# Expert weights in loads of 1 MB with 8 KB rows, expert 1's gather ahead of expert 0's first product, and the turned inner activations copied ahead of the evacuated rows

## The chip, the core and the metric

The kernel runs on one core of a Trainium2 chip. The core has five engines, each with its own queue of instructions: TensorE (PE) for matrix products and transposes, VectorE (DVE), ScalarE (ACT), GpSimd (POOL) and SyncE (SP), which here only issues transfers. Sixteen DMA engines move data between memory and the on-chip buffers. The metric is the time of one execution in microseconds. Before the change it is 886.41 us, the median of three runs (886.3 to 887.85).

## The reference

One layer of a decoder: 512 tokens of width 1024, fp32.

```python
h = layer_norm(x)
proj = h @ w_in                       # nine parts
y_a = hgrn2_branch(...) @ w_branch_a; y_b = stick_breaking_branch(...) @ w_branch_b
h = layer_norm(alpha*h + (sigmoid(gate_a)*y_a + sigmoid(gate_b)*y_b) @ w_mix_out)
h = layer_norm(alpha*h + memory_cross_attention(h, mem, ...))
h = layer_norm(alpha*h + hierarchical_moe(h, ...))

# hierarchical_moe: top-1 of 4 groups, top-2 of the 4 experts in it
for e in range(16):
    hidden = silu(h @ w1[e]) * (h @ w3[e])       # 1024 -> 512
    y = y + combine[:, e:e+1] * (hidden @ w2[e]) # 512 -> 1024
```

The reference lets every expert see every token with a weight that is zero for most; a kernel may compute the chosen tokens alone. One expert has 6 MB of weights in fp32, all sixteen 96 MB.

## The kernel before

The layer runs stage after stage: entry norm and projections, the two branches, their mixing, the cross attention, the experts, the last norm. The change touches the experts, from some 584 us on, and the buffers that weights are loaded into.

**Weights.** The class `Weights` holds a list of loads in the order of their use (`add`) and a list of free buffers (`raw_free`). Whenever a buffer comes free (`buffers`, `done`), `load` issues the next load on SP's queue (L54). A load is 512 KB, 4 KB on each of 128 partitions: for `w1` and `w3` two rows of 2 KB that lie side by side in memory (for expert 0 apart), for `w2` one row of 4 KB. Twelve loads make one expert. The buffers are slots of earlier stages (`raws`, `ring`, `ringout`, `xres`, `sbk`, `wx`, `s`), each given to the list when its stage has done with it. Eight loads can be under way; each further issue waits for the landing of the eighth before it.

**Routing.** For each tile of 128 tokens the router's scores are made (`route_*`), the chosen experts and the places of the tokens in the experts' lists. The tokens of expert 0 are turned by one-hot products (`gather0`, L1129) and copied to `xgT` (L1260). For the others, `count_tokens` (L1272) and `sums` (L1135) make lists of token numbers on PE from one-hot matrices that DVE writes (`one_hots`, L1117); `gather(e)` (L1187) then fetches the rows of expert e's tokens from `x2d` in memory with an indirect DMA of POOL's queue. The rows of the last tile are stored to `x2d` on ACT's queue (L1250), and POOL's queue stores scaled rows to `yd` (`route_base`, L1058), to which the experts' outputs are later added.

**Side work.** `tell()` is a generator of small steps; `begin` puts it beside the products and `tick()` lets it go on after a part of a product. So counting, sums and `gather(1)` stand in the middle of expert 0's first product.

**The loop over experts.** Round e has, in the code's order: `up(e)` (L1451; beyond 64 tokens also L1462), `turn_in(e+1)` (PE L1424, copies L1425 on ACT and DVE), `gather(e+2)`, `down(e-1)` (L1492; beyond 64 tokens L1500), `to_rows(e-1)` and its scatter, and `turn_hidden(e)`: four transposes on PE (L1479) and a copy on DVE (L1481) into the tile that `down(e)` of the next round reads. `to_rows` scales the output out of the product's banks into rows: ACT L1515 twice and L1521 four times, DVE L1523 four times. The rows lie in one buffer (`y_out`), which the scatter (L1301, an indirect DMA with addition, on POOL's queue) reads; the next expert's `to_rows` has to wait until that scatter has landed. Each engine takes its instructions in this order, so what stands behind a waiting instruction waits too.

**The tail.** After expert 15's first product, `yd` is read back (L1559) and added up with the outputs of experts 14 and 15, which are not scattered (L1591, L1624), and the last norm ends the kernel.

Of the kernel before, what the change touches and what calls it, by code (L numbers as in the profile page):

```python
# [24 lines left out]
class Weights:  # L25


    def __init__(self, nc, ahead):
        self.nc, self.ahead = nc, ahead
        self.other = ()  # L30
        self.src, self.raw_free, self.raw, self.parts = [], [], {}, {}
        self.out_free, self.own = [], {}
        self.kept = None
        self.plain = set()
        self.loaded = self.split = 0
        self.limit = 1 << 30
# [8 lines left out]

    def buffers(self, raw=(), out=()):
        self.raw_free += raw
        self.out_free += out
        self.load()

    def load(self):
        while self.raw_free and self.loaded < len(self.src):
            ap, buf = self.src[self.loaded], self.raw_free.pop(0)
            self.nc.sync.dma_start(buf.rearrange("p (k n) -> p k n", n=ap.shape[-1]), ap)  # L54
            self.raw[self.loaded] = buf
            self.loaded += 1

    def prepare(self, upto):
        while self.split <= min(upto, self.limit, len(self.src) - 1):
            j = self.split  # L60
            if not self.out_free:
                return
            hi, lo = self.own[j] = self.out_free.pop(0)
            raw = self.raw.pop(j)
            self.nc.scalar.copy(hi, raw)  # L65
            eng = self.nc.gpsimd if j in self.other else self.nc.vector
            eng.tensor_tensor(lo, raw, hi.bitcast(F32), op=ALU.subtract)  # L67
            n = self.src[j].shape[-1]
            self.parts[j] = tuple(a.rearrange("p (k n) -> p k n", n=n) for a in (hi, lo))
            self.split += 1  # L70
            self.raw_free.append(raw)
            self.load()

    def get(self, j):
        if j in self.plain:
            return self.raw[j]
        self.prepare(j + self.ahead)
        return self.parts[j]

    def done(self, j):  # L80
        if j in self.plain:
            self.raw_free.append(self.raw.pop(j))
# [14 lines left out]
def tile_kernel(ctx, tc, x, mem, ln_in_g, ln_in_b, w_in, hg_lb_logits, hg_norm_g, w_branch_a, w_branch_b,  # L97
# [75 lines left out]
    W.buffers([raws[:, i] for i in range(2)], outs)  # L173
    nc.sync.dma_start(xres[:, 1], x[P:2 * P])
    W.buffers([raws[:, i] for i in (2, 3)])
# [272 lines left out]
    wx = pp.tile([P, 2, T], F32, name="wx")  # L448
    sbk = pp.tile([P, 2, T + 1], F32, name="sbk")
# [263 lines left out]
    W.buffers([sbk.rearrange("p a n -> p (a n)")[:, 0:D]], [out_tile(3)])  # L713
# [176 lines left out]
    def ring(tags):  # L890
        for i in tags:
            r = slot(i, [P, 2, D], name=f"ring{i}")
            rings[i] = [r[:, 0], r[:, 1]]
            W.buffers(rings[i])
# [81 lines left out]
    W.buffers([s8[:, 1], wx.rearrange("p a n -> p (a n)")])  # L976
# [255 lines left out]

    natural_major([q_wo[1]], oc(0), oc(1), ev_wo, before=lambda t: begin(route_first(t), 2))
    for i in range(4):
        r = pp.tile([P, 2, D], F32, tag=f"out{i}", name=f"ringout{i}")
        W.buffers([r[:, 0], r[:, 1]])
# [6 lines left out]
    gather0(0, 0)  # L1243
    gather0(0, 1)
    route_fold(t)
    W.buffers([xres[:, 0]])
# [6 lines left out]
    route_place(slice(t, t + 1))  # L1253
    gather0(3, 0)
    gather0(3, 1)
    s3 = slot(3, [P, 2, D], name="s3")
    W.buffers([s3[:, 1]])
    xgT = s3[:, 0].rearrange("p (k n) -> p k n", n=P)
# [3 lines left out]
    W.buffers([xres[:, 1]])  # L1262
# [123 lines left out]
    route_base(t)  # L1386
    route_told(slice(2, 4))
    one_hots()

    def tell():  # L1390
        count_tokens()
        sums(told[:, 0:NE], [(r, t, k) for r, t in all_rt for k in range(2)])
        nc.vector.tensor_scalar(gidx, told[:, 0:NE], 4096.0, None, op0=ALU.add)
        gather(1)
        yield 1
        W.buffers([xres[:, 2], xres[:, 3]])
        count_blocks()
        nc.vector.tensor_copy(tok, told[:, 0:NE])
        yield 0.5
        yield from route_gates()  # L1400
# [18 lines left out]
    def turn_in(e):  # L1419
        xg = gbr[:, 1].rearrange("t (q p k) -> t q k p", q=4, k=2)  # L1420
        for q in range(2):
            p = msp()
            for i in range(4):
                nc.tensor.transpose(p[:, i * P:(i + 1) * P], xg[:, 2 * q + i // 2, i % 2], ident)  # L1424
# [18 lines left out]
    def up(e):  # L1443
        x, (a, b) = xgT, sums_up
        ws = []
        for q, js in enumerate(q_up[e]):
            ws.append([W.get(j) for j in js])
            for k in range(2):
                c = 2 * q + k
                for i, w in enumerate(reversed(ws[q])):  # L1450
                    nc.tensor.matmul(a[64 * i:64 * i + 64], x[:, c, 0:64], w[:, k * 512:(k + 1) * 512], start=c == 0,  # L1451
                                     stop=c == 7)
            tick()
        if e == 0:
            finish()
        beyond[e] = nc.tensor.value_load(tally[0:1, e:e + 1], min_val=0, max_val=T)

        def part(g):
            for c in range(8):
                for i in range(4):  # L1460
                    o = c % 2 * 512 + i % 2 * 256
                    nc.tensor.matmul(b[32 * i:32 * i + 32, 256 * g:256 * g + 256],  # L1462
                                     x[:, c, 64 + 32 * g:96 + 32 * g], ws[c // 2][i // 2][:, o:o + 256],
                                     start=c == 0, stop=c == 7)
# [11 lines left out]
    def turn_hidden(e, h, p=None):  # L1476
        p = p or msp()
        for i in range(4):
            nc.tensor.transpose(p[:, i * P:(i + 1) * P], h[:, i * P:(i + 1) * P], ident)  # L1479
# [4 lines left out]
    def down(e):  # L1484

        x, (a, b) = hT.pop(e), sums_down
        ws = [W.get(j) for j in q_w2[e]]

        def base():
            for k, w in enumerate(ws):  # L1490
                for n in range(2):
                    nc.tensor.matmul(a[64 * n:64 * n + 64], x[:, k, 0:64], w[:, n * 512:(n + 1) * 512], start=k == 0,  # L1492
                                     stop=k == 3)
                tick()

        def part(g):
            for k, w in enumerate(ws):
                s = slice(64 + 32 * (k // 2), 96 + 32 * (k // 2))
                for i in range(4):
                    nc.tensor.matmul(b[32 * i:32 * i + 32, 256 * g:256 * g + 256], x[:, 2 * g + k % 2, s],  # L1500
                                     w[:, 256 * i:256 * i + 256], start=k == 0, stop=k == 3)
# [24 lines left out]
    for e in range(NE - 1):  # L1526
# [4 lines left out]
        if e == 13:  # L1531
            scratch.extend(W.raw_free.pop() for i in range(4))
            more_blocks()
            W.buffers(scratch)
# [17 lines left out]
    def last_loads():  # L1552

        assert W.loaded == len(W.src)
        whole = [i for i in rings if all(any(b is f for f in W.raw_free) for b in rings[i])][:4]
        free.extend(b for b in W.raw_free if b is not s3[:, 1] and not any(b is h for i in whole for h in rings[i]))
# [50 lines left out]
    yh[NE - 1], yl[NE - 1] = two_parts(3, "yg15")  # L1607
# [3 lines left out]
    p = msp()  # L1611
    for i in range(4):
        nc.tensor.transpose(p[:, i * P:(i + 1) * P], h[:, i * P:(i + 1) * P], ident)
# [7 lines left out]
    ws = [W.get(j) for j in q_w2[NE - 1]]  # L1621
    for n in range(2):
        for k, w in enumerate(ws):
            nc.tensor.matmul(sums_up[n], x[:, k], w[:, halves[n]], start=k == 0, stop=k == 3)  # L1624
# [96 lines left out]
```

## Time and profile before

| | us |
|---|---|
| median of three runs | 886.41 |
| profiled execution | 886.88 |
| its span | 885.1 |
| PE busy | 847.2 (96%) |
| DVE busy | 457.1 (52%) |
| ACT busy | 337.7 (38%) |
| POOL busy | 123.8 (14%) |

The span is what the trace covers; the profiled execution's own time is 1.8 us longer. Mean granted clock of PE: 0.985. Of 177.66 MB moved, 157.31 MB are SP's queue (56144 packets), which is the weights for the most part.

How to read it: a busy engine is not yet the bound, and a wait of an engine that nobody waits for costs nothing. A row of the timeline gives the start and the length of a group of like instructions, and in brackets how long the engine stood idle before it and what ended that. In the rows of stretches, the bracketed counts are instructions, and PEclk is the granted clock as a share of full speed.

### The profile page before, as it was taken

The numbers are of one execution on the slowest core, as the hardware profiler recorded it, in microseconds if no ns is written. First come the engines' busy times: TensorE is split into PE (matmuls) and PEld (weight loads), VectorE is DVE, ScalarE is ACT, GpSimd is POOL, SyncE is SP. The second block draws the span as 40 slices with busy tenths as digits, with TensorE's granted clock in tenths as the row PEclk, the third lists the DMA queues.
The fourth block names the chain that finished last, engine by engine and source line by source line (L and its number), as shares of the span: only waits on it lengthen the run. The fifth ranks groups of instructions, "written<-read, shape, count | busy, mean of one in ns | idle before, by whom it ended". The sixth has DMA issues, their size and how long they took to land. (4 is left out here: it accounts for less than half of the span.)

```text
span 885.1 us, 13705 instructions
## 1 busy us (share of the span) xinstructions
PE 847.2 (96%) x5296; PEld 586.1 (66%) x5296; DVE 457.1 (52%) x806; ACT 337.7 (38%) x640; POOL 123.8 (14%) x212
## 2 busy tenths in 40 slices
PE   6999999999999999999999999997989999999994
PEld 5888777788777777888988888773333343344343
DVE  6632578644558554759744566684242322422336
ACT  2332336543554553422633444222332333323234
POOL 5400000000212220002200000221121111211102
PEclk8999999999999999999999999999999999999998
DMA  8443222222212227332742567599999999999952
GB/s 299 140 135 96 73 93 76 72 72 72 95 48 72 72 78 256 119 118 73 219 167 70 187 220 284 215 351 373 392 378 364 346 350 351 359 360 357 361 172 95
DMA packets 63908, 177.66 MB, mean 201 GB/s; under 512 B 7797, under 2 KB 7829, under 8 KB 63824
## 3 DMA queue, kind: packets, MB, share of 16 engines
q1 hardware_dynamic: 56144, 157.31, 49.6%
q0 software_dynamic: 7536, 18.65, 6.9%
q8 instruction: 60, 0.98, 0.4%
q10 hardware_dynamic: 144, 0.52, 0.1%
q14 instruction: 24, 0.20, 0.1%
HBM read 168.47 MB, written 15.73 MB: 208 GB/s over the span
## 5 line engine op out<-in xcount | busy, mean ns | idle before, releaser
L1523 DVE TENSOR_SCALAR ringgb<-I-5383_acc,wgb 32x256 f32<-32x256 f32 x60 | 29.2, 487 | 118.2 <-ACT ringgb L1521 116.7
L1451 PE MATMUL I-5377_acc<-ring,s 128*64 128x512 f32 x276 | 79.0, 596 | 0.0
L1515 ACT ACTIVATE ringgb<-I-5381_acc,wgb 64x512 f32<-64x512 f32 x30 | 20.5, 684 | 80.8 <-DMA yd<-ringgb,s 64.9
L67 DVE TENSOR_TENSOR I-69_out<-raws,I-69_out 128x1024 fp32r<-128x1024 f32 x24 | 29.4, 1224 | 38.3 <-ACT I-69_out L65 37.9
L1451 PEld LDWEIGHTS I-5377_acc<-ring,s 128*64 128x64 f32 x276 | 23.7, 137 | 34.0 <-issue 31.5
L1301 POOL DMA_INDIRECT yd<-ringgb,s x14 | 22.4, 1600 | 157.1 <-DVE I-8384w2k L1481 16.9
L663 DVE TENSOR_TENSOR_SCAN wx<-sbk 128x128 f32<-128x128 f32 (+3 forms) x32 | 27.1, 847 | 28.7 <-POOL sbk L659 28.7
L65 ACT CAST I-73_out<-raws 128x1024 fp32r<-128x1024 f32 x23 | 24.2, 1050 | 45.5 <-PE I-3558_acc L190 17.1
L67 DVE TENSOR_TENSOR I-71_out<-raws,I-71_out 128x1024 fp32r<-128x1024 f32 x23 | 28.1, 1224 | 24.6 <-ACT I-71_out L65 24.6
L65 ACT CAST I-69_out<-raws 128x1024 fp32r<-128x1024 f32 x25 | 26.3, 1050 | 32.7 <-issue 9.2
L67 DVE TENSOR_TENSOR I-73_out<-raws,I-73_out 128x1024 fp32r<-128x1024 f32 x22 | 26.9, 1223 | 16.1 <-ACT I-73_out L65 15.8
L65 ACT CAST I-71_out<-raws 128x1024 fp32r<-128x1024 f32 x24 | 25.3, 1054 | 24.9 <-PE I-384_acc L189 4.6
L1521 ACT ACTIVATE ringgb<-I-5383_acc,wgb 32x256 f32<-32x256 f32 x60 | 27.9, 464 | 4.3 <-issue 2.2
L1451 PE MATMUL I-5377_acc<-raws,s 128*64 128x512 f32 x60 | 27.8, 601 | 0.0
L659 POOL TENSOR_SCALAR_AFFINE_SELECT sbk<-sbk 128x128 f32<-128x128 f32 x32 | 14.3, 447 | 94.5 <-ACT sbk L654 50.2
L1462 PE MATMUL I-5379_acc<-ring,s 128*32 128x256 f32 x392 | 27.4, 380 | 0.0
L1451 PE MATMUL I-5377_acc<-ringout,s 128*64 128x512 f32 x92 | 25.0, 595 | 0.0
L1187 POOL DMA_INDIRECT ringgb<-x2d,s x15 | 15.7, 1045 | 49.3 <-PE I-5540_ms L1424 8.6
L1462 PEld LDWEIGHTS I-5379_acc<-ring,s 128*32 128x32 f32 x392 | 14.5, 110 | 12.1 <-issue 4.1
L216 POOL TENSOR_TENSOR I-1461hgss<-I-1461hgss,mhalf 128x4 f32<-128x4 f32 x1 | 1.0, 1047 | 136.9 <-DVE I-1461hgss L567 136.9
L966 POOL MEMSET I-4794w2k<- 128x128 f32 x1 | 0.2, 204 | 109.9 <-PE I-4740_ms L190 109.9
L1451 PEld LDWEIGHTS I-5377_acc<-ringout,s 128*64 128x64 f32 x92 | 7.6, 137 | 11.4 <-issue 11.1
(3506 smaller groups left out, 2410.3 us busy)
## 6 DMA issues: line engine op xcount, KB each, us to landing
ring<-in_moe_w_dram SPq DMA_DIRECT2D x107, 512.0 KB, 11.9
raws<-in_w_in_dram SPq DMA_DIRECT2D x44, 512.0 KB, 3.5
ringout<-in_moe_w_dram SPq DMA_DIRECT2D x32, 512.0 KB, 13.2
raws<-in_moe_w_dram SPq DMA_DIRECT2D x20, 512.0 KB, 11.2
xres<-in_moe_w_dram SPq DMA_DIRECT2D x16, 512.0 KB, 13.7
s<-in_moe_w_dram SPq DMA_DIRECT2D x8, 512.0 KB, 13.0
raws<-in_xa_wk_dram SPq DMA_DIRECT2D x7, 512.0 KB, 3.7
raws<-in_xa_wv_dram SPq DMA_DIRECT2D x7, 512.0 KB, 3.7
```

What stands on the lines that cost most here:

```text
L65: self.nc.scalar.copy(hi, raw)
L67: eng.tensor_tensor(lo, raw, hi.bitcast(F32), op=ALU.subtract)
L216: nc.gpsimd.tensor_tensor(o, v, mhalf[:, :v.shape[-1]], op=ALU.pow)
L659: nc.gpsimd.affine_select(kp[:, d], kp[:, d], pattern=[[-1, P]], compare_op=ALU.is_gt, fill=1.0, base=w * (P - 1), channel_multiplier=1 - ...
L663: nc.vector.tensor_tensor_scan(rest[:, :n][:, ::-1], kp[:, n:0:-1], kp[:, n:0:-1], 1.0, ALU.mult, ALU.bypass)
L1187: nc.gpsimd.indirect_dma_start(out=gbr[:, 1], out_offset=None, in_=x2d[:, :], in_offset=bass.IndirectOffsetOnAxis(ap=gidx[:, e:e + 1], axi ...
L1301: nc.gpsimd.indirect_dma_start(out=yd[:, :], out_offset=bass.IndirectOffsetOnAxis(ap=idx, axis=0), in_=y, in_offset=None, bounds_check=T - ...
L1451: nc.tensor.matmul(a[64 * i:64 * i + 64], x[:, c, 0:64], w[:, k * 512:(k + 1) * 512], start=c == 0, stop=c == 7)
L1462: nc.tensor.matmul(b[32 * i:32 * i + 32, 256 * g:256 * g + 256], x[:, c, 64 + 32 * g:96 + 32 * g], ws[c // 2][i // 2][:, o:o + 256], start ...
L1515: nc.scalar.activation(y[0:64, n * 512:(n + 1) * 512], a[s], AF.Copy, scale=gates_at[s, 0, e:e + 1])
L1521: nc.scalar.activation(o, z, AF.Copy, scale=f)
L1523: nc.vector.tensor_scalar(o, z, f, None, op0=ALU.mult)
```

## The change

It has three parts.

**Loads of 1 MB.** The expert weights are loaded in 6 pieces for each expert instead of 12, 8 KB on each partition: for `w1` and `w3` four rows of 2 KB side by side (expert 0's still apart), for `w2` two of 4 KB. 192 loads become 96. Buffers of 2048 columns are given whole, and `halve`, `free` and `room` cut one into two for the loads of other stages that are 4 KB wide, and put two halves together again when both are free. `wx` and `sbk` become one tile. The sum of the buffers stays. The order of rows in a product follows the new layout (`turn_in`, `turned_hidden` take other strides), and `xgT` moves to another slot.

**Expert 1's gather first.** `route_told` and `one_hots` of the last tile come before the copies of `xgT`; `tell()` is driven to its first `yield` before `up(0)`, so that counting, sums and `gather(1)` stand ahead of expert 0's first product, and `route_base` of the last tile, with its two stores to `yd`, comes after the gather.

On POOL, around the last two stores to `yd` of the routing (`yd<-w2k`) and the first gather (`ringgb<-x2d`), the order before is:

```order
L1058 DMA yd<-I-5263w2k 128x512
L1058 DMA yd<-I-5267w2k 128x512
L1265 IOTA wgb 128x48
L1266 IOTA wgb 128x48
L1058 DMA yd<-I-5355w2k 128x512
L1058 DMA yd<-I-5359w2k 128x512
L1187 DMA ringgb<-x2d,s_4897 128x1024
```

and with the change:

```order
L1099 DMA yd<-I-5242w2k 128x512
L1099 DMA yd<-I-5246w2k 128x512
L1308 IOTA wgb 128x48
L1309 IOTA wgb 128x48
L1228 DMA ringgb<-x2d,s_4884 128x1024
L1099 DMA yd<-I-5388w2k 128x512
L1099 DMA yd<-I-5392w2k 128x512
```

The first gather has moved ahead of the last two stores; nothing else on this queue has.

**The copy before the evacuations.** `turn_hidden(e)` stands right behind `down(e-1)`, ahead of `to_rows(e-1)` and the scatter.

On DVE, one round of the loop before; the four `TENSOR_SCALAR` to `ringgb` are the evacuation of `to_rows`, the `COPY` to `w2k` is that of `turn_hidden`, the `COPY` to `s` that of `turn_in`:

```order
L1473 TENSOR_TENSOR I-5896w2k<-I-5896w2k,I-5377_acc 64x512
L1473 TENSOR_TENSOR I-5896w2k<-I-5896w2k,I-5379_acc 64x512
L1425 COPY s_5346<-I-5909_ms 128x512
L1438 UNCONDITIONAL_BRANCH
L1523 TENSOR_SCALAR ringgb<-I-5383_acc,wgb 32x256 x4
L1481 COPY I-5984w2k<-I-5978_ms 128x512
```

and with the change:

```order
L1516 TENSOR_TENSOR I-5859w2k<-I-5859w2k,I-5374_acc 64x512
L1516 TENSOR_TENSOR I-5859w2k<-I-5859w2k,I-5376_acc 64x512
L1466 COPY s_4884<-I-5872_ms 128x512
L1481 UNCONDITIONAL_BRANCH
L1529 COPY I-5932w2k<-I-5926_ms 128x512
L1572 TENSOR_SCALAR ringgb<-I-5380_acc,wgb 32x256 x4
```

The copy of the turned inner activations has passed the evacuation. On PE the four transposes stand behind the down product as before, since the evacuation has nothing on PE.

```diff
 class Weights:
+    def halve(self, wide):
+        if id(wide) not in self.halves_of:
+            a, b = wide[:, 0:1024], wide[:, 1024:2048]
+            self.halves_of[id(wide)] = a, b
+            self.pair[id(a)], self.pair[id(b)] = (wide, b), (wide, a)
+        return self.halves_of[id(wide)]
+    def free(self, buf):
+        wide, other = self.pair.get(id(buf), (None, None))
+        if wide is not None and self.is_free(other):
+            self.raw_free = [b for b in self.raw_free if b is not other] + [wide]
+        else:
+            self.raw_free.append(buf)
+    def room(self, wide):
+        fit = [b for b in self.raw_free if not wide or b.shape[-1] == 2048]
...
+        if wide or fit[0].shape[-1] == 1024:
+            return fit[0]
+        buf, other = self.halve(fit[0])
+        self.raw_free.insert(0, other)
+        return buf
     def load(self):
-        while self.raw_free and self.loaded < len(self.src):
-            ap, buf = self.src[self.loaded], self.raw_free.pop(0)
-            self.nc.sync.dma_start(buf.rearrange("p (k n) -> p k n", n=ap.shape[-1]), ap)
+        while self.loaded < len(self.src):
+            ap = self.src[self.loaded]
+            k, n = ap.shape[1:]
+            buf = self.room(k * n == 2048)
+            if buf is None:
+                return
+            self.nc.sync.dma_start(buf.rearrange("p (k n) -> p k n", n=n), ap)
...
-            q_up[e] = [tuple(W.add(w[0, e, 2 * q * P:(2 * q + 2) * P].rearrange("(k p) n -> p k n", p=P) if e == 0 else
-                                   w[0, e, 2 * q * P:(2 * q + 2) * P].rearrange("(p k) n -> p (k n)", k=2)[:, None], True)
-                             for w in (moe_w1, moe_w3)) for q in range(4)]
+            q_up[e] = [tuple(W.add(w[0, e, 4 * q * P:(4 * q + 4) * P].rearrange("(k p) n -> p k n", p=P) if e == 0 else
+                                   w[0, e, 4 * q * P:(4 * q + 4) * P].rearrange("(p k) n -> p (k n)", k=4)[:, None], True)
+                             for w in (moe_w1, moe_w3)) for q in range(2)]
         if e > 0:
-            q_w2[e - 1] = [W.add(moe_w2[0, e - 1, k * P:(k + 1) * P].rearrange("(k p) n -> p k n", p=P), True)
-                           for k in range(4)]
+            q_w2[e - 1] = [W.add(moe_w2[0, e - 1, 2 * q * P:(2 * q + 2) * P].rearrange("(p k) n -> p (k n)", k=2)[:, None],
+                                 True) for q in range(2)]
...
     route_place(slice(t, t + 1))
+    route_told(slice(2, 4))
+    one_hots()
     gather0(3, 0)
...
-    route_base(t)
-    route_told(slice(2, 4))
-    one_hots()
     def tell():
         count_tokens()
         sums(told[:, 0:NE], [(r, t, k) for r, t in all_rt for k in range(2)])
         nc.vector.tensor_scalar(gidx, told[:, 0:NE], 4096.0, None, op0=ALU.add)
         gather(1)
+        yield 0
+        route_base(t)
+        W.buffers([xrow[1]])
         yield 1
-        W.buffers([xres[:, 2], xres[:, 3]])
         count_blocks()
...
-    begin(tell(), 2)
+    telling = tell()
+    next(telling)
+    begin(telling, 1)
...
     def up(e):
...
+        for c in range(8):
+            for i in range(2):
+                nc.tensor.matmul(a[64 * i:64 * i + 64], x[:, c, 0:64], w(1 - i, c, 0, 512), start=c == 0, stop=c == 7)
+            if c % 2:
+                tick()
...
         if e > 0:
             for step in down(e - 1):
                 step()
+        turn_hidden(e, h)
+        if e > 0:
             finish()
             scatter(to_rows(e - 1), gidx[:, e - 1:e])
-        turn_hidden(e, h)
```

## Rows read from the trace of the kernel before

**Rows 1.** page, part 2: busy tenths in 40 slices of 22.1 us

```profile
PE   6999999999999999999999999997989999999994
...
DMA  8443222222212227332742567599999999999952
```

**Rows 2.** stretches of the expert loop, base products of line 1451 alone

```profile
624.20:666.80 42.60, 21.26 (x96) 6.63 (x96) 0.96 1.01 383
666.80:749.40 82.60, 35.44 (x160) 11.04 (x160) 1.00 0.98 353
749.40:776.20 26.80, 14.18 (x64) 4.42 (x64) 1.00 0.98 358
776.20:835.60 59.40, 21.26 (x96) 6.63 (x96) 1.00 0.99 360
```

**Rows 3.** timeline 589 to 610 us: start, us, engine, line, operation, [idle before <- releaser]

```profile
589.94 0.35 ACTq L1250 DMA_DIRECT2D x2d<-xres  x1
...
595.03 0.69 DVE L1260 COPY s<-I-5280_acc 128x512 f32<-128x512 f32 x1 [2.14 <-PE I-5280_acc L1129]
...
596.04 1.38 DVE L1117 TENSOR_SCALAR I-5366w2k<-s 128x128 bf16<-128x128 bf16 x8
...
599.68 1.11 POOL L1187 DMA_INDIRECT ringgb<-x2d,s  x1 [3.03 <-DVE wgb L1278]
...
607.11 1.13 PE L1424 MATMUL I-5533_ms<-ident,ringgb 128*128 128x128 f32 x4 [4.35 <-DMA ringgb<-x2d,s]
```

**Rows 4.** one stretch, all engines: busy us and count of each, PEclk, DMA, GB/s

```profile
607.00:610.00 3.00, 2.90 (x14) 2.57 (x16) 0.72 (x2) 0.59 (x1) 0.64 (x1) 0.50 1.03 414
```

**Rows 5.** timeline 643 to 667 us, around the down products of experts 2 and 3

```profile
645.44 1.61 POOL L1301 DMA_INDIRECT yd<-ringgb,s  x1 [11.29 <-DVE I-5984w2k L1481]
...
645.65 1.08 PE L1492 MATMUL I-5381_acc<-s,I-5984w2k 128*64 128x512 f32 x4
...
646.55 2.75 PE L1492 MATMUL I-5381_acc<-xres,I-5984w2k 128*64 128x512 f32 x12
...
654.51 1.39 ACT L1515 ACTIVATE ringgb<-I-5381_acc,wgb 64x512 f32<-64x512 f32 x2 [8.43 <-DMA yd<-ringgb,s]
...
655.92 1.93 ACT L1521 ACTIVATE ringgb<-I-5383_acc,wgb 32x256 f32<-32x256 f32 x4
...
657.89 2.04 DVE L1523 TENSOR_SCALAR ringgb<-I-5383_acc,wgb 32x256 f32<-32x256 f32 x4 [10.35 <-ACT ringgb L1521]
...
659.97 0.69 DVE L1481 COPY I-6174w2k<-I-6168_ms 128x512 f32<-128x512 f32 x1
...
660.76 1.36 PE L1492 MATMUL I-5381_acc<-ring,I-6174w2k 128*64 128x512 f32 x4 [2.15 <-issue]
...
663.55 2.56 PE L1492 MATMUL I-5381_acc<-ring,I-6174w2k 128*64 128x512 f32 x8
```

**Rows 6.** timeline 770.5 to 777 us, the down product of expert 10

```profile
771.36 1.22 PE L1492 MATMUL I-5381_acc<-raws,I-7504w2k 128*64 128x512 f32 x3 [0.38 <-ACT s L1425]
...
772.78 2.79 PE L1492 MATMUL I-5381_acc<-ring,I-7504w2k 128*64 128x512 f32 x11
```

**Rows 7.** scatters of line 1301: issue to landing

```profile
DMA to landing us min/median/max: 8.2/9.0/9.9
```

**Rows 8.** DMA from 584 to 842 us: queue, packets, MB, share; then issues

```profile
q1 hardware_dynamic: 22975, 83.67, 84.9%
...
q10 hardware_dynamic: 144, 0.52, 0.5%
...
x2d<-xres ACTq DMA_DIRECT2D x1, 512.0 KB, 7.3
```

**Rows 9.** DMA from 338 to 340.4 us, two queues busy

```profile
q0 software_dynamic: 153, 0.63, 64.0%
q1 hardware_dynamic: 158, 0.32, 37.0%
```

**Rows 10.** DMA issues from 560 to 580 us, KB each, median us to landing

```profile
x2d<-xres POOLq DMA_DIRECT2D x2, 512.0 KB, 3.1
```

More of the change, by code (lines that the diff above doesn't have):

```diff
@@ L172, in tile_kernel @@
     outs = [out_tile(i) for i in range(4)]
-    W.buffers([raws[:, i] for i in range(2)], outs)
+    raw2 = [raws[:, i:i + 2].rearrange("p a n -> p (a n)") for i in (0, 2)]
+    W.buffers([raw2[0]], outs)
     nc.sync.dma_start(xres[:, 1], x[P:2 * P])
-    W.buffers([raws[:, i] for i in (2, 3)])
+    W.buffers([raw2[1]])
     for t in (2, 3):
@@ L447, in tile_kernel @@
     G = slot(10, [P, NT, 512], name="hgG")
-    wx = pp.tile([P, 2, T], F32, name="wx")
-    sbk = pp.tile([P, 2, T + 1], F32, name="sbk")
+    wsb = pp.tile([P, 4 * T + 2], F32, name="wsb")
+    wx = wsb[:, 0:2 * T].rearrange("p (a n) -> p a n", a=2)
+    sbk = wsb[:, 2 * T:4 * T + 2].rearrange("p (a n) -> p a n", a=2)
+    wsb = W.halve(wsb[:, 0:4 * T])
     oTa_h = oTa_l = None
@@ L891, in ring @@
         for i in tags:
-            r = slot(i, [P, 2, D], name=f"ring{i}")
-            rings[i] = [r[:, 0], r[:, 1]]
-            W.buffers(rings[i])
+            rings[i] = slot(i, [P, 2 * D], name=f"ring{i}")
+            W.buffers([rings[i]])
     rings, attended = {}, []
@@ L1231, in tile_kernel @@
     more = take([10], I32, where=1)
+    xrow = [xres[:, t:t + 2].rearrange("p a n -> p (a n)") for t in (0, 2)]
     natural_major([q_wo[1]], oc(0), oc(1), ev_wo, before=lambda t: begin(route_first(t), 2))
     for i in range(4):
-        r = pp.tile([P, 2, D], F32, tag=f"out{i}", name=f"ringout{i}")
-        W.buffers([r[:, 0], r[:, 1]])
+        W.buffers([pp.tile([P, 2 * D], F32, tag=f"out{i}", name=f"ringout{i}")])
     gather0(1, 0)
@@ L1444, in up, with w @@
         x, (a, b) = xgT, sums_up
[L1445 to L1453, printed above, removed]
+        def w(i, c, o, n):
+            return W.cut(q_up[e][c // 4][i], c % 4 * 512 + o, n)
+        for c in range(8):
[3 more added lines that the diff above has]
+                tick()
         if e == 0:
@@ L1486, in down, with w @@
         x, (a, b) = hT.pop(e), sums_down
-        ws = [W.get(j) for j in q_w2[e]]
+        def w(k, o, n):
+            return W.cut(q_w2[e][k // 2], k % 2 * D + o, n)
         def base():
-            for k, w in enumerate(ws):
+            for k in range(4):
                 for n in range(2):
-                    nc.tensor.matmul(a[64 * n:64 * n + 64], x[:, k, 0:64], w[:, n * 512:(n + 1) * 512], start=k == 0,
-                                     stop=k == 3)
+                    nc.tensor.matmul(a[64 * n:64 * n + 64], x[:, k, 0:64], w(k, n * 512, 512), start=k == 0, stop=k == 3)
                 tick()
         def part(g):
-            for k, w in enumerate(ws):
+            for k in range(4):
                 s = slice(64 + 32 * (k // 2), 96 + 32 * (k // 2))
@@ L1531, in tile_kernel @@
         if e == 13:
-            scratch.extend(W.raw_free.pop() for i in range(4))
+            lent = [b for b in W.raw_free if b.shape[-1] == 2048][-2:]
+            W.raw_free = [b for b in W.raw_free if not any(b is i for i in lent)]
+            scratch.extend(h for b in lent for h in W.halve(b))
             more_blocks()
-            W.buffers(scratch)
+            W.buffers(lent)
         if e == 0:
@@ L1554, in last_loads @@
         assert W.loaded == len(W.src)
-        whole = [i for i in rings if all(any(b is f for f in W.raw_free) for b in rings[i])][:4]
-        free.extend(b for b in W.raw_free if b is not s3[:, 1] and not any(b is h for i in whole for h in rings[i]))
+        whole = [i for i in rings if W.is_free(rings[i])][:5]
+        for b in W.raw_free:
+            if not any(b is rings[i] for i in whole):
+                free.extend(W.halve(b) if b.shape[-1] == 2048 else [b])
+        free.append(s8[:, 1])
         for t in (1, 2, 3, 0):
@@ L1606, in tile_kernel @@
     yh[NE - 2], yl[NE - 2] = two_parts(rooms.pop(), "yg14")
-    yh[NE - 1], yl[NE - 1] = two_parts(3, "yg15")
+    yh[NE - 1], yl[NE - 1] = two_parts(rooms.pop(), "yg15")
     base, rest = down(NE - 2)
     base()
-    p = msp()
-    for i in range(4):
-        nc.tensor.transpose(p[:, i * P:(i + 1) * P], h[:, i * P:(i + 1) * P], ident)
+    p = turned_hidden(h)
     x = work("w2k", [P, T], bufs=5).rearrange("p (k n) -> p k n", n=P)
@@ L1620, in tile_kernel @@
     rest()
-    ws = [W.get(j) for j in q_w2[NE - 1]]
     for n in range(2):
-        for k, w in enumerate(ws):
-            nc.tensor.matmul(sums_up[n], x[:, k], w[:, halves[n]], start=k == 0, stop=k == 3)
+        for k in range(4):
+            nc.tensor.matmul(sums_up[n], x[:, k], W.cut(q_w2[NE - 1][k // 2], k % 2 * D + n * T, T), start=k == 0, stop=k == 3)
     for j in q_w2[NE - 1]:
```

52 lines of the change are left out of this document (31 added, 21 removed).

## The prediction

> **What bounds the kernel now.** I read the page's slices first: TensorE (PE) is at nine tenths or more in all slices but four, and from the 27th slice (575 us) to the 38th (841 us) the 16 DMA engines are full too [rows 1]. So two things are nearly bounds in the expert stage, and it is the waits of PE that tell which one ends last. The view by stretches shows how fast PE goes through the experts: 96 base products (32 an expert) in 42.6 us, then 160 in 82.6, 64 in 26.8 and 96 in 59.4 [rows 2]. A round is thus 14.2, 16.5, 13.4 and 19.8 us; the long ones are experts with more than 64 tokens.
>
> PE's own waits are few. Before expert 1 it stands 4.35 us for that expert's gather, issued at 599.68 and landed at about 607.1; in the stretch behind, the granted clock is 0.50, the lower of the two levels (1.2 of 2.4 GHz), until 610 [rows 3, 4]. At 660.76 it has stood 2.15 us ahead of a down product [rows 5]. What ended last there is seen on the other engines: ACT's evacuation waits 8.43 us for the scatter of the expert before, then takes 1.39 + 1.93; DVE's evacuation follows with 2.04, and only then DVE copies the turned inner activations that the down product reads (659.97 + 0.69 = 660.66) [rows 5]. The row names "issue" as the releaser; the copy's end, 0.1 us before the product starts, tells more. A small wait at the same place of the loop, 0.38, stands at 771.36 [rows 6]. These are the waits of the stage that I price.
>
> Behind that lies a loop that PE doesn't see in most rounds: scatter to landing 9.0 (8.2 to 9.9) [rows 7], 1.39 + 1.93 on ACT, 2.04 on DVE, 0.69 for the copy that the scatter also waits for (its releaser is DVE L1481), and some 0.2 of issue: 15.3; from the scatter at 645.44 to the end of the next copy, 660.66, it is 15.2 [rows 5]. In the three rounds up to 666.8 PE without its stalls needs (42.6 - 3.85) / 3 = 12.9 us, so the loop falls behind by 2.4 a round, 7.1 in three, and PE loses 2.15 of it: some 5.0 us of lateness are absorbed. In longer rounds the loop catches up.
>
> **The change, part by part.**
>
> *The copy ahead of the evacuations.* The copy no longer stands behind 2.04 on DVE, and so not behind ACT's 1.39 + 1.93 and the scatter. Both waits of this kind go: 2.15, and 1.70 of clock (the down product behind it takes 663.55 + 2.56 - 660.76 = 5.35 instead of 645.65 to 649.30 = 3.65) [rows 5]; 0.38, and 772.78 + 2.79 - 771.36 - 3.65 = 0.56 [rows 6]. Together **-4.8**. What is late next is the bank of the down product itself: ACT L1515 has to empty it before the next down product writes it. That comes 1.93 + 2.04 + 0.69 = 4.66 earlier than the old condition, so the absorbed lateness rises from 5.0 to about 9.6. The loop loses the copy's 0.69: 14.6 at unchanged landings. If an expert beyond 64 tokens follows, the second bank has to be emptied too, but such rounds are the long ones.
>
> *Expert 1's gather.* Its indices are there some 3 us earlier, since counting and sums stand before expert 0's first product instead of in its middle. PE's own work is only moved. On DVE the eight one-hots (1.38) and two smaller operations now come before the copy at 595.03, which had 2.14 of idle time before it [rows 3]: that hides them; without that cover the first product would start up to 1.9 later. But the gather also needs the last rows of its source, stored from ACT's queue at 589.94 and 7.3 us on the way [rows 3, 8]: not before 597.2. The gain is 599.68 - 597.2 = 2.4, if nothing else moves, and 0.7 of the clock if the wait shrinks (the four transposes times three at half clock). The two stores to yd that it passes on POOL's queue start about 2 us later; the first scatter, at 630, is the first to need them.
>
> *Packets of 8 KB.* The loads go from 192 to 96 and each row from 4 to 8 KB. In a stretch with two queues busy, 153 packets of 4 KB took 64.0% of 16 x 2.4 us, 161 ns each, and 158 of 2 KB 37.0%, 90 ns each [rows 9]. By the same slope 8 KB is an estimate of 303 ns, so a weight byte is up to 6% cheaper. Weights are 84.9% of the DMA time from 584 to 842 [rows 8], so the stream could end up to 12 us earlier. PE does not wait for it in any row, so I value that at 0 (bounds: 0, and a lead that lets nothing run late).
>
> The price is paid by the others. In that same stretch the two queues advance nearly one packet for one (153 to 158). A gather, a scatter or the store has eight rows and an end packet on each DMA engine (the store's queue shows 144 packets on 16 engines [rows 8]); nine turns, each longer by 303 - 161 = 142 ns, are **+1.3** us to landing. From below: 0, if long rows are moved in pieces of 4 KB. From above: the store took 3.1 us with the weights mostly idle and 7.3 beside them [rows 8, 10], 4.2 more; nine turns of 161 ns explain 1.45, the other 2.75 is time until its first packet. If that lag is a number of packets already handed over, it grows too, by 2.75 x 142/161 = 2.4: **+3.8** in all. The trace shows no lag behind larger packets, so this is open. I take 1.3, since rows 9 show the turns and nothing shows that the lag is counted in packets.
>
> With 1.3, the gather: -2.4, +1.3 for the store, +1.3 for itself: **+0.2**, and no clock back. The loop: 14.6 + 1.3 = 15.9 against 12.9 loses 3 a round, 9 in three, just inside 9.6; five rounds of 16.5 give 3.3 back; two of 12.9 (26.8 less 0.94 of stall) add 6: 11.7, so about **+2** of wait near 775; the long rounds clear the rest before the tail. Sum: -4.8 + 0.2 + 2 = -2.6 on the profiled 886.88, which lies 0.5 above the median of the runs: 884.2. I say **884.0**.
>
> The Trainium skill speaks against this part. "DMA: Bandwidth & Descriptors", section "Queues, rings and completion order", says that a DMA engine drains a whole packet of typically 9 to 17 descriptors from one ring before it turns to the next. By that rule a gather would wait out not nine single rows but one batch of 9 to 17, an estimate of 1.3 to 2.4 us more with rows of 8 KB, instead of my 1.3. Rows 9, equal counts over 2.4 us, fit single rows better, but do not show the order within one engine.
>
> **Rivals.**
>
> *Landings stay (rows moved as before).* For: nothing in the trace shows an 8 KB weight row. Then -4.8 - 2.4 - 0.7 = -7.9: **879.0**. The loop of 14.6 loses 1.7 a round in the short ones and is absorbed. Against: rows 9 show that a 4 KB packet takes 1.8 times a 2 KB one, so size does count.
>
> *The scatter loop becomes the bound: slower.* Place: ACT L1515 waiting for the scatter, and behind it PE L1492 waiting for its bank. The point from which it decides is a landing of about 10.5 us, where -4.8 - 2.4 + 2 x 1.55 and some 4 of waits cancel. In a middle case, +1.85 a landing (where the quoted rule would also put it), the loop is 16.4: 3 x 3.5 - 9.6 = 0.9 over, 9.1 left after the five, + 7 - 9.6 = 6.5 over: 7.4 of waits, -4.8 + 1.3 + 7.4 = +3.9: **891**. With the lag counted in packets the loop is 18.4: 6.8 over in the first three, 5 x 1.9 and 2 x 5.5 more, 27; -4.8 + 5.2 + 27: **914**. For: the store's 7.3 against 3.1. Against: that lag may be bytes or time.
>
> *The weights end last: no change.* If 8 KB rows move no faster per byte, the stream, which has the DMA engines full from 575 on [rows 1], ends where it ended. PE's lead over it stands in no row, and it now waits for pieces of 1 MB: with a lead near zero in the last experts, what PE saves elsewhere is waited for there. **886**. For: that full row. Against: 90 ns for 2 KB and 161 for 4 KB.
>
> **How the numbers follow.** Landings +1.3: 0.47, its own range 880 to 888. Landings as before: 0.13. Middle case: 0.15. Lag in packets: 0.17. Weights last: 0.08. The range 878 to 905 leaves out a little of the case at 879 and the larger part of the case at 914, which begins near 898. A measurement of this kernel tells about 0.2% from no change, 1.8 us. Faster: 0.13 + 0.26 of the likeliest + 0.03 of the middle and the weights = 0.42. Same: 0.14 + 0.02 + 0.05 = 0.21. Slower: 0.07 + 0.12 + 0.17 + 0.01 = 0.37.
>
> **What would show it.** The copy: no PE wait at the place of 660.76, clock full there, and the DVE copy right behind the transposes. The gather: issued at 597 to 599, PE still waiting 4 to 5 us for it; landing at the old 607 would confirm the +0.2. The packets: loads of 1 MB on the page, packet count of the weight queue halved, scatters landing in a median of 10.3. If that median is 9.0, the first rival holds; at 11 or more PE L1492 will show waits in the short rounds near 650 and 770, and I am wrong in sign. If PE L1451 waits on a weight tile, the last rival holds.

## The result, and the profile after

The changed kernel takes 896.94 us (median of six runs, 893.26 to 898.33) where the kernel before takes 887.76 in the same runs: a ratio of 1.0098, 95% interval 1.0082 to 1.0114. It is slower. The forecast was 884.0, faster; the time lies in the range of 878 to 905, but on the other side of the kernel before.

The slices of the changed kernel's page answer to [rows 1]; the third line is the granted clock, which the first group did not show:

```profile
PE   6999999999999999999999999979989998799994
...
PEclk8999999999999999999999999998989999899998
DMA  8432222212222244424731574898999999998242
```

The granted clock of the kernel before:

```profile
PEclk8999999999999999999999999999999999999998
```

PE is still at nine tenths nearly everywhere, the DMA engines are still full for most of the expert stage, and the clock has dents that it did not have. PE's waits of the expert stage, with their total, count and longest, say why:

```profile
PE I-7521_ms L1465 <- DMA ringgb<-x2d,s: 5.2, 1, 5.2
PE I-5506_ms L1465 <- DMA ringgb<-x2d,s: 4.1, 1, 4.1
PE I-6233_ms L1465 <- DMA ringgb<-x2d,s: 3.7, 1, 3.7
PE I-7337_ms L1465 <- DMA ringgb<-x2d,s: 1.8, 1, 1.8
PE I-7153_ms L1465 <- DMA ringgb<-x2d,s: 0.9, 1, 0.9
```

L1465 is `turn_in`, the old L1424. Before, the only such wait was expert 1's, 4.35 [rows 3]; now experts 5, 10, 11 and 12 wait too, 3.7 + 0.9 + 1.8 + 5.2 = 11.6 us. What happens at the first of them is seen in the timeline around it, which answers to [rows 5] (L1344 scatter, L1228 gather, L1564 and L1570 the evacuation on ACT, L1572 that on DVE, L1542 the down product, L1516 the product of the hidden halves on DVE):

```profile
646.51 1.61 POOL L1344 DMA_INDIRECT yd<-ringgb,s  x1 [12.70 <-DVE I-6043w2k L1516]
...
648.42 1.03 POOL L1228 DMA_INDIRECT ringgb<-x2d,s  x1 [0.30 <-issue]
...
656.90 1.39 ACT L1564 ACTIVATE ringgb<-I-5378_acc,wgb 64x512 f32<-64x512 f32 x2 [11.09 <-DMA yd<-ringgb,s]
...
658.32 1.93 ACT L1570 ACTIVATE ringgb<-I-5380_acc,wgb 32x256 f32<-32x256 f32 x4
...
660.28 2.05 DVE L1572 TENSOR_SCALAR ringgb<-I-5380_acc,wgb 32x256 f32<-32x256 f32 x4 [9.64 <-ACT ringgb L1570]
...
660.64 1.10 PE L1465 MATMUL I-6233_ms<-ident,ringgb 128*128 128x128 f32 x4 [3.71 <-DMA ringgb<-x2d,s]
...
662.36 0.68 DVE L1516 TENSOR_TENSOR I-6227w2k<-I-6227w2k,I-5374_acc 64x512 f32<-64x512 f32 x1
...
662.52 5.25 PE L1542 MATMUL I-5378_acc<-ring,I-6116w2k 128*64 128x512 f32 x16
...
663.10 1.59 POOL L1344 DMA_INDIRECT yd<-ringgb,s  x1 [13.65 <-DVE I-6227w2k L1516]
```

The gather is issued at 648.42, right behind a scatter that was itself late (646.51), and PE gets its rows at 660.64, 3.71 late. The scatter's landing (656.9) is what the evacuation waits for, as before. The 2.15 us at the old place, ahead of the down product, are gone: that copy is no longer in the way. But the transposes and the down product behind the new wait run from 660.64 to 667.77, 7.13 us, against 644.25 to 649.03, 4.78, in the round before. Two stretches, columns as in [rows 4]:

```profile
660.60:668.00 7.40, 7.20 (x25) 3.10 (x25) 3.69 (x7) 1.44 (x3) 2.63 (x2) 0.65 1.01 419
779.00:787.00 8.00, 7.72 (x25) 3.23 (x26) 3.14 (x6) 0.88 (x2) 2.63 (x2) 0.61 0.97 353
```

The granted clock is 0.65 and 0.61 there: 2.4 us are lost behind the first long wait and 2.8 behind the second (779.12 to 786.74, 7.62 us for the same work). So 11.6 + 2.4 + 2.8 = 16.8 of new cost against 4.8 saved: 12.0; the span has grown by 896.6 - 885.1 = 11.5. (These are the two profiled executions; the changed kernel's is the slowest of its six runs, and the medians differ by 9.2.)

The landings grew, and not all by the same amount. The changed kernel from 600 to 842 us (queue: packets, MB, share; then issues with the median us to landing):

```profile
q1 hardware_dynamic: 10844, 78.89, 81.9%
...
ringgb<-x2d,s POOLq DMA_INDIRECT x14, 11.9
yd<-ringgb,s POOLq DMA_INDIRECT x13, 10.3
```

and the kernel before in the same stretch:

```profile
q1 hardware_dynamic: 21771, 79.26, 85.7%
...
ringgb<-x2d,s POOLq DMA_INDIRECT x15, 8.1
```

Scatters went from 9.0 [rows 7] to 10.3, as forecast. Weight packets are half as many, and a megabyte takes 0.819 x 3872 / 78.89 = 40.2 engine-us instead of 0.857 x 3872 / 79.26 = 41.9: 4.0% less. But gathers went from 8.1 to 11.9. A single gather right behind a scatter, after and then before:

```profile
ringgb<-x2d,s POOLq DMA_INDIRECT x1, 12.1
```

```profile
ringgb<-x2d,s POOLq DMA_INDIRECT x1, 9.6
```

and one that stands further behind a scatter (5.4 and 4.5 us), after and then before:

```profile
ringgb<-x2d,s POOLq DMA_INDIRECT x1, 8.7
```

```profile
ringgb<-x2d,s POOLq DMA_INDIRECT x1, 7.2
```

Such a gather lost 1.5, about as much as a scatter; right behind a scatter on the same queue it lost 2.5. These are single pairs; over all gathers issued within 2.6 us of a scatter the medians are 12.1 after and 9.6 before. And because scatters are later now, nine gathers stand that close behind one, where three did before.

Expert 1's gather, which answers to [rows 3]:

```profile
588.62 0.34 ACTq L1291 DMA_DIRECT2D x2d<-xres  x1
...
598.60 1.13 POOL L1228 DMA_INDIRECT ringgb<-x2d,s  x1 [10.80 <-DMA x2d<-xres]
...
605.27 1.12 PE L1465 MATMUL I-5506_ms<-ident,ringgb 128*128 128x128 f32 x4 [4.09 <-DMA ringgb<-x2d,s]
```

The store at 588.62 took 9.1 to land (7.3 before [rows 8]), the gather was issued 1.1 us earlier than before and not 2.4, and PE still waits 4.09 us for it. The store itself went out 1.3 us earlier than in the trace before (588.62 against 589.94).

### The profile page after: what moved, and what is told of

Its sections match the earlier page's. It is cut to its first block, busy times and chain, and to the rows that moved or that the text cites. A ratio compares the mean times of both kernels' runs of the same rounds, so it can differ in the third digit from the quotient of the medians.

```text
span 896.6 us, 13517 instructions
## 1 busy us (share of the span) xinstructions
PE 851.8 (95%) x5296; PEld 589.0 (66%) x5296; DVE 456.8 (51%) x806; ACT 338.0 (38%) x640; POOL 123.8 (14%) x212
## 5 line engine op out<-in xcount | busy, mean ns | idle before, releaser
L1495 PE MATMUL I-5374_acc<-ring,s 128*64 128x512 f32 x312 | 97.6, 606 | 0.0
L1572 DVE TENSOR_SCALAR ringgb<-I-5380_acc,wgb 32x256 f32<-32x256 f32 x60 | 29.2, 487 | 83.2 <-ACT ringgb L1570 81.7
L1564 ACT ACTIVATE ringgb<-I-5378_acc,wgb 64x512 f32<-64x512 f32 x30 | 20.5, 684 | 117.6 <-DMA yd<-ringgb,s 109.1
L1495 PEld LDWEIGHTS I-5374_acc<-ring,s 128*64 128x64 f32 x312 | 29.5, 139 | 40.2 <-issue 38.6
L1344 POOL DMA_INDIRECT yd<-ringgb,s x14 | 22.3, 1593 | 184.5 <-DVE ringgb L1572 38.5
L705 DVE TENSOR_TENSOR_SCAN wsb<-wsb 128x128 f32<-128x128 f32 (+3 forms) x32 | 27.1, 847 | 28.7 <-POOL wsb L701 28.7
L1505 PE MATMUL I-5376_acc<-ring,s 128*32 128x256 f32 x416 | 30.7, 380 | 0.0
L1570 ACT ACTIVATE ringgb<-I-5380_acc,wgb 32x256 f32<-32x256 f32 x60 | 27.9, 464 | 3.2 <-issue 1.1
L1495 PE MATMUL I-5374_acc<-ringout,s 128*64 128x512 f32 x88 | 28.5, 596 | 0.0
L1495 PE MATMUL I-5374_acc<-raws,s 128*64 128x512 f32 x64 | 28.5, 595 | 0.0
L1505 PEld LDWEIGHTS I-5376_acc<-ring,s 128*32 128x32 f32 x416 | 16.2, 110 | 12.8 <-issue 4.1
L1228 POOL DMA_INDIRECT ringgb<-x2d,s x15 | 15.7, 1047 | 41.0 <-DMA x2d<-xres 10.8
```

Of the source, the lines that this page charges most:

```text
L705: nc.vector.tensor_tensor_scan(rest[:, :n][:, ::-1], kp[:, n:0:-1], kp[:, n:0:-1], 1.0, ALU.mult, ALU.bypass)
L1228: nc.gpsimd.indirect_dma_start(out=gbr[:, 1], out_offset=None, in_=x2d[:, :], in_offset=bass.IndirectOffsetOnAxis(ap=gidx[:, e:e + 1], axi ...
L1344: nc.gpsimd.indirect_dma_start(out=yd[:, :], out_offset=bass.IndirectOffsetOnAxis(ap=idx, axis=0), in_=y, in_offset=None, bounds_check=T - ...
L1495: nc.tensor.matmul(a[64 * i:64 * i + 64], x[:, c, 0:64], w(1 - i, c, 0, 512), start=c == 0, stop=c == 7)
L1564: nc.scalar.activation(y[0:64, n * 512:(n + 1) * 512], a[s], AF.Copy, scale=gates_at[s, 0, e:e + 1])
L1570: nc.scalar.activation(o, z, AF.Copy, scale=f)
```

## The experiments

All ratios are to the kernel before in the same runs, with 95% intervals. "The moves" are the copy ahead of the evacuations and expert 1's gather first. Theory A: rows of 8 KB lengthen the turns of gathers and scatters, and the gather queued on POOL behind the scatter is where PE pays.

**The moves without the new loads (e1).**

```diff
...
+    route_told(slice(2, 4))
+    one_hots()
     gather0(3, 0)
...
+    telling = tell()
+    next(telling)
+    begin(telling, 1)
...
+        turn_hidden(e, h)
+        if e > 0:
             finish()
             scatter(to_rows(e - 1), gidx[:, e - 1:e])
```

> The kernel before with the two moves alone (copy ahead of the evacuations, expert 1's gather first); the loads stay at 512 KB with 4 KB rows. Theory A (rows of 8 KB lengthen each turn that gathers and scatters wait for, and the gather that stands behind a scatter on POOL's queue makes PE wait): scatters land in a median of 9.0 as before, gathers right behind a scatter in 9.5, PE has no wait for a gather after expert 1; the stalls of 2.15 and 0.38 with their clock go and the first gather comes 2.4 earlier: 880 to 883. Rival B (the moves themselves cost, because the scatter and the gather behind it come later): 890 or more, with PE waiting for gathers in the short rounds.

Measured: 884.05, ratio 0.9963 (0.9950 to 0.9976). Landings from 600 to 842 us:

```profile
ringgb<-x2d,s POOLq DMA_INDIRECT x14, 9.5
yd<-ringgb,s POOLq DMA_INDIRECT x14, 9.1
```

No wait for a gather is left after expert 1's. So the moves do no harm (B falls), but they bring 3 us where I counted 4 to 7. PE's waits show what took the rest:

```profile
PE I-5396_acc L1453 <- DMA ring<-in_moe_w_dram: 3.2, 2, 2.4
...
PE I-5396_acc L1627 <- ACT I-8521w2k L1620: 1.9, 1, 1.9
```

L1453 is the base product of expert 12: its weights come too late. L1627 is the last product, behind the read of `yd`.

**The copy alone (e2)** and **the gather alone (e3)**, the single parts of the edit above.

> The kernel before with the copy ahead of the evacuations alone. Theory A: the waits at 660.76 and 771.36 and the half clock behind them go, -4.8: 883. The scatter's issue stays 0.77 us after the last evacuation on DVE, so the loop of scatters stays at 15.3. Rival B: 888 or more.

Measured: 887.8, ratio 1.0009 (0.9996 to 1.0021): nothing. The waits at the old places are gone, yet:

```profile
PE I-5377_acc L1625 <- ACT I-8521w2k L1618: 2.2, 1, 2.2
PE I-5377_acc L1451 <- DMA ring<-in_moe_w_dram: 2.1, 1, 2.1
```

The 2.1 are expert 12's weights again, the 2.2 the last product, with `yd`'s read landing late (0.6 at that place in the kernel before). What the copy saves is waited for again at the weights and at the last product. A missed expectation, and the same limit as in e1.

> The kernel before with expert 1's gather ahead of expert 0's first product alone. Theory A: the gather is issued when the store of the last rows has landed, 2.4 earlier; the stalls of the copy stay at their places, and the loop of scatters sets the pace through the short rounds: 884 to 887. Rival B: 888 or more.

Measured: 884.78, ratio 0.9960 (0.9944 to 0.9975). As expected; with rows of 4 KB the whole gain of the moves is there with the gather alone.

**The new loads without the moves (e4).** The two moves undone in the changed kernel.

> The changed kernel with both moves undone: loads of 1 MB with 8 KB rows alone. Theory A: scatters 10.3, gathers behind a scatter 12, loop 16.5; the copy behind the evacuations stalls the down products too: 897 to 905. Rival B: the packets do no harm, 886 or less.

Measured: 899.65, ratio 1.0146 (1.0126 to 1.0166). As expected: the loads cost 1.5%; the moves give about 0.5% of it back. Its trace shows the same chain without the moves: scatters land in 10.3, gathers right behind one in 12, and PE waits 2.6 and 3.9 us for the gathers of experts 5 and 12.

**Loads of 1 MB, rows of 4 KB (e5).**

```diff
...
-                                   w[0, e, 4 * q * P:(4 * q + 4) * P].rearrange("(p k) n -> p (k n)", k=4)[:, None], True)
+                                   w[0, e, 4 * q * P:(4 * q + 4) * P].rearrange("(j p k) n -> p j (k n)", j=2, k=2), True)
...
```

(and `w2`, `turn_in` and `turned_hidden` to match)

> The changed kernel with its loads of 1 MB and its buffers, but two rows of 4 KB on each partition that lie apart in memory instead of one of 8 KB. Theory A (the length of a row counts): landings as before the change, 9.0 and 9.5, no PE wait for gathers in the short rounds, 880 to 884. Rival C (the size of a load, what is under way at once and the coarser buffers count): landings 10.3 and 12, 895 to 898 as the changed kernel.

Measured: 888.45, ratio 1.0018 (1.0007 to 1.0030): neither. Landings from 600 to 842 us:

```profile
q1 hardware_dynamic: 20409, 78.64, 85.3%
...
ringgb<-x2d,s POOLq DMA_INDIRECT x14, 9.8
yd<-ringgb,s POOLq DMA_INDIRECT x13, 9.6
```

They lie between those of e1 and of the changed kernel. Scatters go 9.1, 9.6, 10.3, so about half of what they lost comes with the larger loads and half with the longer row. Gathers issued within 2.6 us of a scatter go 9.55, 10.2, 12.1 in the median: there most of it, 1.9 of 2.5, is the row's. The time of this kernel is lost elsewhere, at expert 12's weights, which now come in pieces of 1 MB without the gain per byte (0.853 x 3872 / 78.64 = 42.0):

```profile
PE I-5374_acc L1495 <- DMA ring<-in_moe_w_dram: 5.8, 2, 4.7
```

**Shorter rows (e8).** e1 with `w1` and `w3` in rows of 2 KB.

> The kernel before with both moves, and w1 and w3 in rows of 2 KB instead of 4 (w2 stays at 4). Theory A (each turn of a gather or scatter waits for one row of the weights): by the mix of rows a turn is some 57 ns shorter; scatters land in 8.5 instead of 9.0, gathers right behind a scatter in 8.5 to 8.7 instead of 9.5; the weights cost more per byte, PE waits for them from expert 11 on: 890 to 905. Rival C (not the row but the load's size counts): landings 9.0 and 9.5.

Measured: 894.53, ratio 1.0064 (1.0042 to 1.0085). Landings:

```profile
ringgb<-x2d,s POOLq DMA_INDIRECT x14, 8.6
yd<-ringgb,s POOLq DMA_INDIRECT x13, 8.9
```

The time lies in the range that was expected, the landings do not. Scatters take 8.9 where 8.5 was expected (9.1 in e1). The 8.6 is the median of all gathers; the seven issued within 2.6 us of a scatter take 9.2, against 9.55 in e1 and 8.5 to 8.7 expected. Shorter rows make landings shorter, but by less than half of what a turn for each row would give.

**Gathers one round earlier (e6),** with a second buffer taken from the ring of weights.

```diff
-    W.buffers([W.halve(xrow[0])[1]])
+    gbuf = [xres[:, 1]]
...
-        if e + 2 < NE:
-            gather(e + 2)
+        if e + 3 < NE:
+            gather(e + 3)
```

> The changed kernel with a second buffer for gathered rows (half of the xres slot, which the ring of weights loses with its other half: 1 MB of 22): each gather is issued one round earlier, so a gather that lands 12 us after a late scatter still has a round to spare. Theory A: the PE waits for gathers (5.2, 3.7, 1.8, 0.9) and the half clock behind the long ones, about 16 us in all, go; scatters keep their 10.3 and the loop its 16.6; what is left is a wait at the down product's bank in the short rounds or for expert 12's weights: 878 to 886. Rival D (PE waits because the loop of scatters as such is too slow, wherever the gather stands): 893 or more.

Measured: 888.91, ratio 1.0009 (0.9999 to 1.0020): some 8 us better than the changed kernel, though not as low as expected. PE's waits:

```profile
PE I-5508_ms L1467 <- DMA ringgb<-x2d,s: 2.9, 1, 2.9
PE I-5380_acc L1544 <- ACT ringgb L1566: 2.7, 3, 1.1
PE I-7400_ms L1525 <- DVE I-7333w2k L1518: 1.6, 1, 1.6
PE I-7530_ms L1467 <- issue: 1.6, 1, 1.6
PE I-6296_ms L1525 <- DVE I-6229w2k L1518: 1.3, 1, 1.3
...
PE I-5380_acc L1544 <- ACTq L1338: 0.5, 1, 0.5
```

Apart from expert 1's no wait for a gather is left, with rows of 8 KB and landings of 10.4 and 11.9. That shows that PE paid most of the loss through the gathers. What is left are the waits that the forecast had named: the down product's bank (L1544), and engines held up behind the scatters; the loop of scatters is 16.2 to 17.6 us long.

**The same with rows of 4 KB (e7).**

> The kernel before with both moves and the early gathers, 4 KB rows and loads of 512 KB. Theory A: there was no PE wait for gathers of later experts to remove; what holds this kernel is the weight stream at expert 12 (landed at 778.9 with the moves alone), and the ring is 512 KB smaller: 883 to 887, as the moves alone or a little slower. Rival D: 880 or less.

Measured: 885.37, ratio 0.9967 (0.9951 to 0.9982), as the moves alone: with 4 KB rows there was no gather to wait for.

**The evacuation divided by banks (e10, e9, e11).** In all kernels so far DVE's evacuation starts when ACT's has ended, though they write different rows: both read the same accumulator bank, and the program runs them one after the other. Now DVE empties one bank, ACT the other; they still write the same buffer of rows.

```diff
-            nc.scalar.activation(y[0:64, ...], a[s], AF.Copy, scale=gates_at[s, 0, e:e + 1])
+            nc.vector.tensor_scalar(y[0:64, ...], a[s], gates_at[s, 0, e:e + 1], None, op0=ALU.mult)
...
-                if i < 2:
-                    nc.scalar.activation(o, z, AF.Copy, scale=f)
-                else:
-                    nc.vector.tensor_scalar(o, z, f, None, op0=ALU.mult)
+                nc.scalar.activation(o, z, AF.Copy, scale=f)
```

e10 is the changed kernel with this alone:

> The changed kernel with the divided evacuation alone, gathers as in the changed kernel. Theory A: the loop is 15.1 and scatters fall behind PE by 2.2 a short round instead of 3.7; the waits for gathers behind a scatter shrink from 11.6 to at most 4 us: 882 to 889. Rival D (the gather's 12 us to landing is too long whatever the loop): 893 or more.

Measured: 883.52, ratio 0.9960 (0.9946 to 0.9975), 1.4% under the changed kernel and as fast as the best of the others. Its timeline (L1564 DVE, L1569 ACT):

```profile
653.03 1.53 DVE L1564 TENSOR_SCALAR ringgb<-I-5378_acc,wgb 64x512 f32<-64x512 f32 x2 [2.00 <-DMA yd<-ringgb,s]
653.04 3.90 ACT L1569 ACTIVATE ringgb<-I-5380_acc,wgb 32x256 f32<-32x256 f32 x8 [6.83 <-DMA yd<-ringgb,s]
...
657.22 1.59 POOL L1344 DMA_INDIRECT yd<-ringgb,s  x1 [10.06 <-ACT ringgb L1569]
...
658.77 3.65 PE L1542 MATMUL I-5378_acc<-ring,I-6116w2k 128*64 128x512 f32 x16
```

and the longest of PE's waits:

```profile
PE I-5506_ms L1465 <- DMA ringgb<-x2d,s: 4.3, 1, 4.3
PE I-5378_acc L1542 <- DVE I-7515w2k L1516: 0.8, 1, 0.8
```

DVE and ACT now start together on the scatter's landing, which shows that it was the shared bank that kept them apart, and the next scatter goes out 4.2 us later instead of 663.10 - 656.90 = 6.2. (Of the 2.0 us 0.5 is the step from the last evacuation to the scatter, which is shorter behind ACT.) The loop is 14.5 to 15 in the short rounds, and no gather but expert 1's holds PE up. Scatters still take 10.2, and the one gather issued 1.9 us behind a scatter, at 659.12, still takes 12.1; but the scatters now go out earlier against PE, two gathers instead of nine stand within 3 us of one, and the median gather takes 9.2. So the longer rows are still paid for in each transfer, and PE waits for none of it.

e9 adds the early gathers, e11 is e1 with the division:

> The changed kernel with the early gathers and with the evacuation divided by banks: DVE empties the base product's bank (two 64x512), ACT the bank of the further tokens (eight 32x256), so that the two no longer stand one behind the other. Theory A: the loop of scatters is landing 10.3, ACT 8 x 0.48 = 3.9 and 0.9 to the issue: 15.1 instead of 16.6; the bank waits that the early gathers left (2.7, 1.6, 1.3 and the transposes at half clock) go, and PE is held by expert 12's weights alone, which land at about 775: 879 to 884, under the kernel before. Rival E (DVE, which now waits for the scatter's landing itself, holds up the copies behind it): 888 or more.

> The kernel before with both moves and the divided evacuation, loads of 512 KB with 4 KB rows. Theory A: loop 13.8, no wait for scatters or gathers in the short rounds; but these waits were already gone with the moves, and PE waits for expert 12's weights, which land at 778 to 779 as before: 882 to 885, no gain on the moves alone.

Measured: e9 887.1, ratio 1.0002 (0.9991 to 1.0013); e11 886.43, ratio 0.9987 (0.9970 to 1.0005). Both miss what was expected of them. In e9 nothing after expert 1 waits for gathers, but the ring is 1 MB smaller, and expert 12's weights are late:

```profile
PE I-5376_acc L1497 <- DMA ring<-in_moe_w_dram: 2.0, 1, 2.0
```

In e10, with the whole ring, PE waits 0.4 us at that place. With the loop short, earlier gathers have nothing to give; that their buffer is all that they cost is not shown. Why e11 is not as fast as e1 is not settled; its profile shows 1.9 us of waits for weights and 2.7 at the last product.

## Why the prediction was wrong

*The sign fell with one step:* "What is late next is the bank of the down product itself". What was late next was the gather. On POOL's queue it stands behind the scatter, so it inherits the scatter's lateness, and its landing grew by 2.5 where a gather further behind a scatter lost 1.5. The margin could have been read: in the kernel before the gather behind the scatter of 645.44 landed at 647.36 + 9.6 = 656.95, and PE took it at 657.41. There were 0.5 us of room; I had no term for this wait, and took 9.6 us of lateness as absorbed. I looked at what the moved copy had hidden on DVE and not at the other queue that hangs on the same scatter. e6 shows it: with the gathers a round earlier the waits for them are gone, and the bank waits that I had forecast are what is left. That 897 lies inside the range is no merit of this mechanism: the range was held wide for the bank and for a lag counted in packets, and neither is what happened.

*The loop "loses the copy's 0.69":* wrong. The page names DVE L1481 as the releaser of the scatter [rows 5]; in the changed kernel it names DVE L1516 in most rounds. In both the scatter goes out 0.77 after the end of DVE's last evacuation (645.44 and 663.10), and so it does where DVE does nothing else in between and the profile names the evacuation itself:

```profile
811.57 2.04 DVE L1572 TENSOR_SCALAR ringgb<-I-5380_acc,wgb 32x256 f32<-32x256 f32 x4 [3.53 <-ACT ringgb L1570]
...
814.38 1.59 POOL L1344 DMA_INDIRECT yd<-ringgb,s  x1 [10.22 <-DVE ringgb L1572]
```

In the other rounds the named instruction happened to end in that gap. So the loop grew to 663.10 - 646.51 = 16.6 and not 15.9, and lost 3.7 a short round instead of 3. Nor did the five longer rounds give 3.3 back: the five loops from 663.10 to 746.98 took 16.8 each, so the scatters stayed late until the second group of short rounds.

*The price of a turn:* the size of +1.3 was met by scatters, and nearly by a gather further behind one, +1.5 (7.2 to 8.7), but in part by luck: by e5 only about half of the scatters' 1.3 comes with the longer row, and by e8 rows of 2 KB take off 0.2 where the same count of turns gave 0.5. That larger loads alone add some 0.5 was in no term. What the sum missed altogether is the gather right behind a scatter, +2.5. Twice nine turns of 142 ns would give that, the scatter's and its own, but no run shows that it is made up so, and by e5 0.6 of it comes with the larger loads. The lag "counted in packets" (+3.8) is not seen: the store lost 1.8. The rule on batches of descriptors that I had quoted from the Trainium skill ("DMA: Bandwidth & Descriptors", "Queues, rings and completion order") would have given an estimated 1.3 to 2.4 for each transfer. The measured 1.3 and 1.5 lie at its lower end, and less with the larger loads' part taken off, so these runs don't decide between it and single rows.

*The copy, -4.8:* the waits went, as said, but e2 is not faster. The value 0 for the weights was wrong: I wrote that PE waits for them in no row, and did not know how close it was. In the kernel before the last weights of expert 12's first product land at 776.4, just as the product starts, about 5 us before it comes to them. e1 and e2 reach that product some 6 us earlier in their traces (1.4 and 3.6 of it were there when the last rows were stored to `x2d`), and PE waits 3.2 and 2.1 us. So the wait that the rival "the weights end last" (0.08) named is seen in every kernel with 4 KB rows and one of the moves, though e1 and e3 gain 0.4% in spite of it; in the changed kernel itself it is not what costs.

*The gather of expert 1, +0.2:* the sum is near what was said, its terms are not. The gather is issued 1.1 earlier, but the store that it waits for went out 1.3 earlier by itself, so the move gave nothing: the store took 1.8 longer, not 1.3, and the gather went out 0.9 after it had landed. The gather itself landed in 6.6 us, against 7.4 before, not 1.3 later. PE had its rows 1.8 us earlier than before, and lost 1.4 of that again behind the wait, at a granted clock of 0.57 from 605.2 to 612.2. With 4 KB rows it is the part that pays, 0.4%.

*The rivals:* "the scatter loop becomes the bound" had the right direction, the loop's 16.4 in the middle case and 891 of the 897, but the wrong place, the bank instead of the gather.

## What to carry to other kernels

Before a change that makes transfers slower, list every instruction on every queue that stands behind the slowed one, and read its margin to its reader; a margin of half a microsecond is not visible in any wait. When a landing grows, compare transfers that stand equally close behind another one: a median over all of them also moves with how many stand so. Where PE, the DMA engines and a loop of dependent transfers all end within a few us, taking a stall from one of them pays only up to the next. And a loop through memory is cheaper to shorten in its engine part than in its transfer: here dividing the evacuation by banks made the longer rows harmless.

## What the runs showed of the hardware

- A scatter issued by POOL goes out 0.77 us after the last evacuation when that is on DVE (663.10 against 660.28 + 2.05), and 0.28 after it when it is on ACT (657.22 against 653.04 + 3.90 in e10). Which instruction the profile names as releaser says little at that distance.
- After waits of 3.7 and 5.2 us PE's next 7.4 and 8.0 us ran at a granted clock of 0.65 and 0.61; after waits of 0.9 and 1.8 the next 5 us ran at 1.00.
- With rows of 8 KB a weight byte took 4.0% less DMA time than with 4 KB.
- Beside the weights, a gather issued within 2.6 us of a scatter on the same queue landed in a median of 9.55 us with loads of 512 KB and rows of 4 KB, 10.2 with 1 MB and rows of 4 KB, and 12.1 with 1 MB and rows of 8 KB (e1, e5, the changed kernel).
